# Three quads of eight by seven products in the down projection, with a second set of buffers for the sums of weights

## The chip, the cores and the metric

One core of a Trainium2 chip runs the whole layer in one launch. The metric is the device time in microseconds (us): the median of three runs before the change is 1021.38 us (1021.27 to 1021.45). Engines are named as the profile names them: PE multiplies matrices (PEld is its weight load), DVE is the vector engine, ACT the scalar engine, POOL is GpSimd, SP issues most DMAs. Each engine works through its own instructions in order and waits at semaphores for the others.

## The reference, cut to what matters

A decoder layer in float32 for 256 tokens and a model width of 2048: attention heads and a pooling mixer behind one norm, then a gated MLP with 5632 hidden features. The change concerns the last product of the MLP:

```python
def conv_ffn(h, w_up, conv_w, conv_b, w_down):
    u = h @ w_up
    ...
    gate, val = jnp.split(y, 2, axis=-1)
    return (jax.nn.silu(gate) * val) @ w_down
```

Here `w_down` is 5632 x 2048, and the product is the "down projection"; `h @ w_up` is the "up projection".

## The kernel before, in words

**Three passes per product.** A float32 weight is cut into a high and a low part, both of a type that PE multiplies in one pass. ACT copies the high part (`wh`, L124), DVE subtracts it from the raw weight and keeps the rest (`wl`, L129). Each product is then three matmuls: high by high, high by low, low by high. Every weight of the layer passes through these two copies, so ACT and DVE work all the time for PE.

**Steps.** The work is a list of steps, and each step uses up one half chunk of weights, 128 x 1024. A chunk of 1 MB holds two steps; SP loads it into one of four `raw` buffers, and the next load starts when a buffer is released (`release`, L160). The order of all instructions is written out by the loop at the end of `layer`: at step u it emits the high split of step u + 6 and the low split of step u + 5, and then the matmuls of step u and the actions hooked to it. For a step that belongs to a quad by sums (below) the matmuls come first and the splits after. So on DVE's queue the low split of a step stands five steps ahead of its matmuls, and everything that is emitted between them stands in line with it.

**MLP in thirds.** The hidden features are worked in three thirds of 8, 8 and 6 groups of 256. Of each third first the up projection: per group a gate block and a value block of four steps each, and after the last step of a block DVE and ACT evacuate it (`conv`, L657: `fs`, `u`, `y`), the value block also multiplies by the gate and cuts the result into `hid` (`value`, L679). Then the down projection of that third: two pairs (`down_pair`, L708), each for 1024 of the 2048 output columns.

**Quads.** In a pair, two steps h = 0 and h = 1 form a quad j: two row blocks of 128 hidden features by two column blocks of 512, for two halves of 128 tokens. By the plain way (`quad`, L744) that is eight products, 24 matmuls of 128x512 in two steps of 12. Quads named in `MIXED` go by seven products of sums (`quad_sums`, L727): 12 matmuls in the first step, 9 in the second. These need sums of the tokens' side (`token_sums`, L690: four additions on POOL, a copy on ACT, a subtraction on DVE, into `sx`), formed with the value block of that group, and sums of the weights:

- `seven_sums` (L139), emitted behind the low split of the quad's first step: ACT copies the first 512 columns into `s512h`, DVE makes `s512l` (L150) and then three differences in the raw chunk (L143, L144, L145), the later ones from the earlier.
- One step later `seven_high` has ACT copy the last sum into `s1024h`, and two steps later `seven_low` (L155) has DVE make `s1024l` (L157) and release the chunk.

The high and low parts of these sums are the tiles `s1` (512 wide) and `s4` (1024 wide), one of each before the change. PE reads `s1024l` with the sixth matmul of the quad, and for the last time with the last matmul of its second step.

**PSUM.** The pair's plain sums lie in two `acc` tiles (`box["tok"]`), the seven products in one `aux` tile (two banks, only one buffer exists) and two `small` tiles p5 and p7 (two buffers exist). Behind the last quad by sums, `add_part` 0 to 4 (L778) combine them into `x2`: 0 and 2 copy with ACT (L783) and add in PSUM (L784), 1 and 3 (L786, L789) read `aux`, 4 (L792) reads p5. Behind the last step `close` (L795, L797) adds both `acc` tiles into `x2`. The next pair starts in the same buffers: its first matmul writes `aux`, its fourth group of three writes the `small` buffer that `add_part` 4 has read, and its second step writes the first `acc` tile, which the first copy of `close` has read.

In the third of 8 before the change, quads 0 and 4 go by sums, in the third of 6 quad 0.

Of the kernel before, what the change touches and what calls it, by code (L numbers as in the profile page):

```python
# [25 lines left out]
F32 = mybir.dt.float32  # L26
F32R = mybir.dt.float32r
# [4 lines left out]
P = 128  # L32
# [22 lines left out]
OK = (0, 2, 4, 6, 12, 14, 8, 10)  # L55
V_TILES = [((k, 0), (k, 1)) for k in range(KT - 2)] + [((KT - 2, b), (KT - 1, b)) for b in range(2)]
THIRDS = ((0, 8), (8, 16), (16, 22))
MIXED = {8: (0, 4), 6: (0,)}


def bucket(n):
# [9 lines left out]
def layer(ctx: ExitStack, tc: tile.TileContext, xT, xtok, wts, par, rel_d, ident_d, icnt_d, out):  # L71
    nc = tc.nc
# [20 lines left out]
    def col(c):  # L93
        return pv[:, c:c + 1]


    raws, wparts, shift, late = {}, {}, {}, {}
    seven = set()

    def load(c, pieces=1, j=0):  # L100

# [8 lines left out]
    def raw(u):  # L110
        return raws[u // 2][:, (u % 2) * HALF:(u % 2 + 1) * HALF]
# [27 lines left out]
    def seven_sums(u):  # L139

        w = raws[u // 2]
        both(late["s1"], w[:, :512])
        nc.vector.tensor_tensor(w[:, :1024], w[:, 512:1536], w[:, :1024], op=OP.subtract)  # L143
        nc.vector.tensor_tensor(w[:, 1024:1536], w[:, 1024:1536], w[:, :512], op=OP.subtract)  # L144
        nc.vector.tensor_tensor(w[:, 1536:], w[:, 1536:], w[:, 1024:1536], op=OP.subtract)  # L145

    def both(parts, w, low=True):
        nc.scalar.activation(parts[0], w, AF.Copy)
        if low:
            nc.vector.tensor_tensor(parts[1], w, parts[0].bitcast(F32), op=OP.subtract)  # L150

    def seven_high(u):
        both(late["s4"], raw(u + 1), low=False)

    def seven_low(u):  # L155
        h, l = late["s4"]
        nc.vector.tensor_tensor(l, raw(u + 1), h.bitcast(F32), op=OP.subtract)  # L157
        release(u // 2)

    def release(c):  # L160

        raws.pop(c)
        if c + RAWS < wts.shape[0]:
            load(c + RAWS)
# [334 lines left out]
    steps, hooks = [], []  # L499
# [29 lines left out]
    def feat_block(act, post, alloc=acc):  # L529
        box, runs = {}, []  # L530
        for i, k0 in enumerate(XK):
            def run(u, i=i, k0=k0):
                if i == 0:
                    box["ps"] = alloc("ps_feat")
                feat_half(u, act(), k0, box["ps"], i == 0, i == 3)
                if i == 3:
                    post(box["ps"])
            run.shift = SHIFT
            runs.append([run])
        return runs  # L540

    def after(u, f):

        hooks.append((u, f))
# [22 lines left out]
    for b in range(2):  # L567
# [4 lines left out]
        for j in range(4):  # L572
            h, u = 4 * b + j, at + 2 * j
# [5 lines left out]
            after(at + 7, lambda: st.__setitem__(("T", 1), bias_tile(4)))  # L579


    def open_late():
        ectx.close()
        pool = ctx.enter_context(tc.tile_pool(name="late", bufs=1))
        late["pool"] = pool
        late["x2"] = pool.tile([P, NT, D], F32, name="x2")
        nc.sync.dma_start(late["x2"], xtok)
        late["sx"] = pool.tile([P, 2, 4, 2, P], F32R, name="sx")
        late["s1"], late["s4"] = ([pool.tile([P, n], F32R, name=f"s{n}{p}") for p in "hl"] for n in (512, 1024))
        late["ss"] = pool.tile([P, NT, D // 512], F32, name="ss")  # L590
        late["u"] = [pool.tile([P, 2, 2 + S], F32, name=f"u{i}") for i in range(2)]
        for u in late["u"]:
            nc.gpsimd.memset(u[:, :, :2], 0.0)
# [6 lines left out]
    def residual(ps, b):  # L600
        for t in range(NT):
            x2 = add_to_x2(ps, b, t)
            sq = late["pool"].tile([P, 512], F32, name="xs", tag="y0", bufs=2)
            nc.scalar.activation(sq, x2, AF.Square, accum_out=late["ss"][:, t, b:b + 1])

    def x2_T(b):
# [49 lines left out]

    def conv(ps, f0_, which):  # L657

        pool, u = late["pool"], late["u"][which]
        s = pool.tile([P, 2, S], F32, name="fs", tag="fs", bufs=2)  # L660
        add_halves(s, ps)
        nc.vector.tensor_tensor(u[:, :, 2:], s, late["rrow"][:, None, :].to_broadcast([P, 2, S]), op=OP.mult)  # L662
        y = pool.tile([P, 2, S], F32, name="y", tag=f"y{which}", bufs=2)
        for m in range(2):
            f = f0_ + m
            cw = [col(C_CW + i * 2 * NF + f) for i in range(3)]
            nc.scalar.activation(y[:, m, :], u[:, m, 2:], AF.Identity, scale=cw[2], bias=col(C_CB + f))  # L667
            nc.vector.scalar_tensor_tensor(y[:, m, :], u[:, m, 1:1 + S], cw[1], y[:, m, :],  # L668
                                           op0=OP.mult, op1=OP.add)
            nc.vector.scalar_tensor_tensor(y[:, m, :], u[:, m, :S], cw[0], y[:, m, :],  # L670
                                           op0=OP.mult, op1=OP.add)
        return y
# [6 lines left out]
    def value(ps, g, j):  # L679
        if j == 0:  # L680
            late["hid"] = keep.tile([P, KT, 2, S], F32R, name="hid", tag="c")
        y = conv(ps, NF + 2 * g, 1)
        hid, ks = late["hid"], slice(2 * j, 2 * j + 2)
        nc.vector.tensor_tensor(y, y, late["gate"], op=OP.mult)  # L684
        nc.scalar.activation(hid[:, ks, 0, :], y, AF.Copy)  # L685
        nc.vector.tensor_tensor(hid[:, ks, 1, :], y, hid[:, ks, 0, :].bitcast(F32), op=OP.subtract)
        if j in late["mixed"]:
            token_sums(y, late["mixed"].index(j))
# [14 lines left out]
    def triple(ps, act, w, first, last, skip=False):  # L703

        for n, (a, i) in enumerate(((0, 0), (1, 0), (0, 1))):
            nc.tensor.matmul(ps, act[a], w[i], start=(first and n == 0), stop=(last and n == 2), skip_group_check=skip)  # L706

    def down_pair(bp, nq, final):  # L708


        box, runs, mixed = {}, [], MIXED[nq]
        s_end = 2 * mixed[-1] + 1
        rest = 2 * nq - 1 - s_end

        def hid(k, t):
            return [late["hid"][:, k, a, t * P:(t + 1) * P] for a in range(2)]
# [10 lines left out]
        def quad_sums(u, j, h):  # L727
            if j == 0 and h == 0:
                box["aux"], box["p5"], box["p7"] = aux("ps_p"), small("ps_p5"), small("ps_p7")
                box["tok"] = [acc("ps_down") for t in range(NT)]  # L730
            first, last, i = j == 0, j == mixed[-1], mixed.index(j)
            if h == 0:
                s4, t13 = late["s4"], wparts.pop(u + 1)
                triple(box["aux"][:, 0, :], hid(2 * j, 0), late["s1"], first, last)
                triple(box["aux"][:, 1, :], sums(i, 1), part(s4, 0), first, last)
                triple(box["p5"], sums(i, 0), part(t13, 0), first, last)
                triple(box["p7"], sums(i, 2), part(t13, 1), first, last)
            else:
                b2, s4 = wparts.pop(u - 1), late["s4"]
                triple(bank(0, 1), sums(i, 3), part(b2, 0), first, False, end)  # L740
                triple(bank(0, 0), hid(2 * j + 1, 0), part(b2, 1), first, False, end)
                triple(bank(1, 0), hid(2 * j + 1, 1), part(s4, 1), first, False, end)
# [60 lines left out]
        for j in range(nq):  # L803
            for h in range(2):
                at = 2 * j + h

                def run(u, j=j, h=h, at=at):
                    if j in mixed:
                        quad_sums(u, j, h)
                    elif end and j == nq - 1:  # L810
                        if h == 1:
                            last_quad((u - 1, u), j)
                    else:
                        quad(u, j, h)
                run.seven = j in mixed and h == 0
                acts = [run]
                for n in range(5):
                    if at == s_end + 1 + n * (rest - 1) // 5:
                        acts.append(lambda n=n: add_part(n))
                if at == 2 * nq - 1 and not end:  # L820
                    acts.append(lambda: close(0))
                runs.append(acts)
        return runs

    for n, (g0, g1) in enumerate(THIRDS):
        after(len(steps), lambda nq=g1 - g0: late.__setitem__("mixed", MIXED[nq]))
        for g in range(g0, g1):
            steps += feat_block(lambda: late["h"], lambda ps, g=g: gate(ps, g), aux if n and g == g0 else acc)
            steps += feat_block(lambda: late["h"], lambda ps, g=g, j=g - g0: value(ps, g, j))
        for bp in range(2):  # L830
            steps += down_pair(bp, g1 - g0, n == len(THIRDS) - 1)

    for u, f in hooks:
        steps[u].append(f)
    n = len(steps)
    assert n == 2 * wts.shape[0], (n, wts.shape)
    shift.update((u, getattr(steps[u][0], "shift", 0)) for u in range(n))
    seven.update(u for u in range(n) if getattr(steps[u][0], "seven", False))
    for u in range(n):
        ahead = u + AHEAD + 1  # L840
        pair = (ahead, ahead + 1) if ahead in PAIRS else ()
# [88 lines left out]
```

## Time and profile before

| what | value |
|---|---|
| median of 3 runs | 1021.38 us |
| the profiled execution's own time | 1021.83 us |
| its span, first to last instruction | 1020.0 us |
| busy: PE, DVE, ACT, POOL | 1015.4, 762.5, 542.9, 61.4 us |
| first matmul of the down projection of third 1, 2, 3 | 472.87, 734.76, 952.26 us |

The profile is of one execution. A row of the timeline gives the start in us from the span's start, the duration, the engine, the line, what is written and read, and how many equal instructions follow each other; in brackets stands how long the engine was idle before, and what ended that. Matmuls overlap each other by their fill: a matmul shows 0.39 us and the next one starts 0.23 us later, so PE's work is read from starts, not from durations. The same holds to a smaller degree on DVE. The chain of work gives pieces by their ends, so a start there can lie 0.16 us behind the one in the timeline.

### The profile page before, as it was taken

How to read it: one execution, taken by the hardware profiler on the slowest of the kernel's cores; microseconds unless marked ns; L12 is line 12 of the kernel's file. 1: busy time of each engine (PE TensorE's matmuls, PEld its weight loads, DVE VectorE, ACT ScalarE, POOL GpSimd, SP SyncE). 2: the span in 40 equal slices, each digit the busy share in tenths (PEclk: the TensorE clock that was granted, in tenths of full speed). 3: DMA queues.
4: the chain of work that ended last, by engine and by line, in shares of the span. 5: the costliest groups of instructions: out<-in, count | busy, mean ns of one | idle time of the engine just before them, and what ended most of it. 6: DMA issues, size and time to landing. Idle time of an engine off the chain costs nothing.

```text
span 1020.0 us, 13506 instructions
## 1 busy us (share of the span) xinstructions
PE 1015.4 (100%) x5286; PEld 872.0 (85%) x5286; DVE 762.5 (75%) x958; ACT 542.9 (53%) x729; POOL 61.4 (6%) x74
## 2 busy tenths in 40 slices
PE   9999999999999999999999999999999999999998
PEld 8888888888888888888888888888888888888887
DVE  6956667875567877878987687777889667777893
ACT  6744455554545565555544465555554445564740
POOL 0420004600000000000000000000000000000000
PEclk9999999999999999999999999999999999999999
DMA  9784454475453555444655445546365555445451
GB/s 340 271 281 167 167 182 165 166 289 200 172 181 137 219 196 213 170 166 169 244 212 201 165 177 218 184 169 238 126 249 209 206 178 188 171 173 218 177 216 41
DMA packets 30607, 199.18 MB, mean 195 GB/s; under 512 B 3576, under 2 KB 4472, under 8 KB 7760
## 3 DMA queue, kind: packets, MB, share of 16 engines
q1 hardware_dynamic: 29968, 196.89, 52.7%
q0 software_dynamic: 576, 1.44, 0.7%
q8 instruction: 41, 0.67, 0.3%
q14 instruction: 22, 0.18, 0.0%
HBM read 195.83 MB, written 2.49 MB: 194 GB/s over the span
## 4 chain that ended last, share of the span: by engine, by line
PE 100%; DVE 0%; issue 0%
PE ps_feat L185 35%; PE ps_feat L187 18%; PE ps_down L750 18%; PE ps_tok L172 17%; PE ps_v L179 4%; PE ps_p L706 3%; PE ps_down L706 2%; PE ps_pool L194 1%; PE ps_s L400 1%; PE ps_start L247 0%; PE ps_down L771 0%; PE ps_T L387 0%; PE ps_x2T L615 0%; PE ps_av L433 0%; PE ps_eT L422 0%; PE ps_av L434 0%
## 5 line engine op out<-in xcount | busy, mean ns | idle before, releaser
L129 DVE TENSOR_TENSOR wl<-raw,wh 128x1024 fp32r<-128x1024 f32 x358 | 436.0, 1253 | 80.0 <-PE ps_tok L172 27.7
L185 PE MATMUL ps_feat<-x2h,wh 128*128 128x512 f32 x1408 | 488.6, 392 | 0.0
L124 ACT ACTIVATE wh<-raw 128x1024 fp32r<-128x1024 f32 x358 | 362.1, 1051 | 159.1 <-DVE raw L143 44.2
L187 PE MATMUL ps_feat<-x2h,wl 128*128 128x256 f32 x1408 | 393.6, 280 | 0.0
L185 PEld LDWEIGHTS ps_feat<-x2h,wh 128*128 128x128 f32 x1408 | 264.3, 188 | 58.3
L187 PEld LDWEIGHTS ps_feat<-x2h,wl 128*128 128x128 f32 x1408 | 264.3, 188 | 0.1
L750 PE MATMUL ps_down<-wh,hid 128*128 128x512 f32 x528 | 130.4, 389 | 0.0
L750 PEld LDWEIGHTS ps_down<-wh,hid 128*128 128x128 f32 x528 | 99.1, 188 | 20.6
L667 ACT ACTIVATE y<-u,pv 128x256 f32<-128x256 f32 x88 | 48.2, 595 | 70.6 <-DVE u L662 70.6
L750 PE MATMUL ps_down<-wl,hid 128*128 128x512 f32 x264 | 70.6, 389 | 0.0
L172 PE MATMUL ps_tok<-wh,xh 128*128 128x512 f32 x256 | 70.1, 396 | 0.0
L172 PE MATMUL ps_tok<-wh,cat 128*128 128x512 f32 x256 | 68.8, 390 | 0.0
L668 DVE SCALAR_TENSOR_TENSOR y<-u,pv,y 128x256 f32<-128x256 f32 x88 | 42.4, 482 | 29.6 <-ACT y L667 29.6
L450 DVE TENSOR_TENSOR fs<-ps_feat,fs 128x512 f32<-128x512 f32 x44 | 30.4, 691 | 38.1 <-ACT fs L449 38.1
L750 PEld LDWEIGHTS ps_down<-wl,hid 128*128 128x128 f32 x264 | 49.6, 188 | 10.3
L172 PEld LDWEIGHTS ps_tok<-wh,cat 128*128 128x128 f32 x256 | 47.6, 188 | 9.6
L172 PEld LDWEIGHTS ps_tok<-wh,xh 128*128 128x128 f32 x256 | 47.5, 188 | 9.4
L449 ACT ACTIVATE fs<-ps_feat 128x512 f32<-128x512 f32 x44 | 26.2, 595 | 44.6 <-PE ps_feat L187 44.4
L185 PE MATMUL ps_feat<-xh,wh 128*128 128x512 f32 x128 | 46.2, 402 | 0.0
L670 DVE SCALAR_TENSOR_TENSOR y<-u,pv,y 128x256 f32<-128x256 f32 x88 | 42.7, 485 | 3.1
L699 POOL TENSOR_TENSOR s<-y 128x128 f32<-128x128 f32 x10 | 6.0, 597 | 629.8 <-DVE y L684 629.8
L685 ACT ACTIVATE hid<-y 128x512 fp32r<-128x512 f32 x22 | 14.0, 634 | 49.0 <-DVE y L684 49.0
(173 smaller groups left out, 904.4 us busy)
## 6 DMA issues: line engine op xcount, KB each, us to landing
raw<-in_wts SPq DMA_DIRECT2D x177, 1024.0 KB, 4.9
raw<-in_wts SPq DMA_DIRECT2D x4, 512.0 KB, 7.9
x<-in_xtok SPq DMA_DIRECT2D x1, 2048.0 KB, 9.6
raw<-in_wts SPq DMA_DIRECT2D x7, 256.0 KB, 5.5
xboth<-in_xT SPq DMA_DIRECT2D x4, 256.0 KB, 6.9
T<-band POOLq DMA_DIRECT2D x8, 128.0 KB, 7.8
out<-x SPq DMA_DIRECT2D x2, 512.0 KB, 6.4
out<-x SPq DMA_DIRECT2D x3, 256.0 KB, 2.2
```

The lines of the kernel that those rows point to most:

```text
L124: nc.scalar.activation(wparts[u][0], raw(u - 1 if u - 1 in seven else u + 1 if u in seven else u), AF.Copy)
L129: nc.vector.tensor_tensor(wl, raw(u - 1 if u - 1 in seven else u + 1 if u in seven else u), wh.bitcast(F32), op=OP.subtract)
L172: nc.tensor.matmul(ps[:, t, :], act[:, k0 + k, a, t * P:(t + 1) * P], w[:, k * 512:(k + 1) * 512], start=(first and k == 0 and n == 0), st ...
L179: nc.tensor.matmul(ps[:, t, :], act[:, k, a, t * P:(t + 1) * P], w[i], start=(first and n == 0), stop=(last and n == 2))
L185: nc.tensor.matmul(ps, wh[:, ws], act[:, k, :, :], start=(first and n == 0), stop=False, skip_group_check=True)
L187: nc.tensor.matmul(ps[:, S:], wl[:, ws], act[:, k, 0, :], start=False, stop=(last and n == len(ks) - 1), skip_group_check=True)
L450: nc.vector.tensor_tensor(dst, ps[:, :, :S], dst, op=OP.add)
L667: nc.scalar.activation(y[:, m, :], u[:, m, 2:], AF.Identity, scale=cw[2], bias=col(C_CB + f))
L668: nc.vector.scalar_tensor_tensor(y[:, m, :], u[:, m, 1:1 + S], cw[1], y[:, m, :], op0=OP.mult, op1=OP.add)
L670: nc.vector.scalar_tensor_tensor(y[:, m, :], u[:, m, :S], cw[0], y[:, m, :], op0=OP.mult, op1=OP.add)
L706: nc.tensor.matmul(ps, act[a], w[i], start=(first and n == 0), stop=(last and n == 2), skip_group_check=skip)
L750: nc.tensor.matmul(bank(t, b), hid(2 * j + h, t)[a], part(w, b if h == 0 else 1 - b)[i], start=(t == b == 1 and j == 1 and h == 0 and n == ...
```

## The change

In thirds of 8 the quads 0, 3 and 5 now go by seven products (before 0 and 4), in the third of 6 quads 0 and 3 (before 0). There are now two sets of `s1` and `s4`, used in turn. The second set has its place in a pool "temps" which during the up projection holds the temporaries `fs`, `y` and `xs`, and which is closed and opened anew at each passage from up to down projection and back. `sx` holds three quads' token sums in place of two. The scratch area for POOL's DMAs is half as large. The five `add_part` calls stand between the last quad by sums and the last step: before in steps 10 to 14 of 16 (third of 6: steps 2 to 10 of 12), now in steps 12, 12, 13, 13, 14 (third of 6: steps 8, 8, 9, 9, 10).

```diff
-MIXED = {8: (0, 4), 6: (0,)}
+MIXED = {8: (0, 3, 5), 6: (0, 3)}
...
     def seven_sums(u):
 
         w = raws[u // 2]
-        both(late["s1"], w[:, :512])
+        both(late["s"][seven[u]][0], w[:, :512])
...
     def seven_high(u):
-        both(late["s4"], raw(u + 1), low=False)
+        both(late["s"][seven[u]][1], raw(u + 1), low=False)
...
+    def seven_tiles(pool, i):
+        return [[pool.tile([P, n], F32R, name=f"s{n}{p}{i}") for p in "hl"] for n in (512, 1024)]
+
+    def open_temps(down):
+
+        if "ctx" in late:
+            late["ctx"].close()
+        late["ctx"] = ExitStack()
+        late["temps"] = late["ctx"].enter_context(tc.tile_pool(name="temps", bufs=1))
+        if down:
+            late["temps"].tile([P, 72], F32, name="row")
+            late["s"][1] = seven_tiles(late["temps"], 1)
...
-        late["sx"] = pool.tile([P, 2, 4, 2, P], F32R, name="sx")
-        late["s1"], late["s4"] = ([pool.tile([P, n], F32R, name=f"s{n}{p}") for p in "hl"] for n in (512, 1024))
+        late["sx"] = pool.tile([P, 3, 4, 2, P], F32R, name="sx")
+        late["s"] = [seven_tiles(pool, 0), None]
+        open_temps(False)
...
-                run.seven = j in mixed and h == 0
+                run.seven = (len(mixed) * bp + mixed.index(j)) % 2 if j in mixed and h == 0 else None
...
+        after(len(steps) - 1, lambda: open_temps(True))
         for bp in range(2):
             steps += down_pair(bp, g1 - g0, n == len(THIRDS) - 1)
+        after(len(steps) - 1, lambda n=n: open_temps(False) if n < len(THIRDS) - 1 else late["ctx"].close())
...
-    nc = bacc.Bacc("TRN2", target_bir_lowering=False, num_devices=1, dynamic_dma_scratch_size=8192)
+    nc = bacc.Bacc("TRN2", target_bir_lowering=False, num_devices=1, dynamic_dma_scratch_size=4096)
```

By the built programs, PE has 18 matmuls fewer (5243 to 5225), DVE 33 additions and subtractions more, ACT 15 copies more and POOL 12 additions more.

On DVE, third 1, first pair, directly behind the evacuation of the last value block (`hid`): the low splits of steps 5 and following, and the sums of the second quad by sums. Before:

```order
L686 TENSOR_TENSOR hid<-y,hid 128x2x256
L129 TENSOR_TENSOR wl<-raw,wh 128x1024 x4
L150 TENSOR_TENSOR s512l<-raw,s512h 128x512
L143 TENSOR_TENSOR raw<-raw 128x1024
L144 TENSOR_TENSOR raw<-raw 128x512
L145 TENSOR_TENSOR raw<-raw 128x512
L129 TENSOR_TENSOR wl<-raw,wh 128x1024 x2
L157 TENSOR_TENSOR s1024l<-raw,s1024h 128x1024
L129 TENSOR_TENSOR wl<-raw,wh 128x1024 x5
```

The same place now, on to the sums of the third quad by sums (`s512l_4133` and `s1024l_4135` are the second set, `s512l_1872` and `s1024l_1874` the first):

```order
L700 TENSOR_TENSOR hid<-y,hid 128x2x256
L129 TENSOR_TENSOR wl<-raw,wh 128x1024 x2
L150 TENSOR_TENSOR s512l_4133<-raw,s512h_4132 128x512
L143 TENSOR_TENSOR raw<-raw 128x1024
L144 TENSOR_TENSOR raw<-raw 128x512
L145 TENSOR_TENSOR raw<-raw 128x512
L129 TENSOR_TENSOR wl<-raw,wh 128x1024 x2
L157 TENSOR_TENSOR s1024l_4135<-raw,s1024h_4134 128x1024
L129 TENSOR_TENSOR wl<-raw,wh 128x1024 x2
L150 TENSOR_TENSOR s512l_1872<-raw,s512h_1871 128x512
```

The sums for the second quad stand two low splits earlier than before, and one more set of sums follows.

On DVE, the end of the same pair: from the sums for the next pair's first quad to `close`. Before:

```order
L150 TENSOR_TENSOR s512l<-raw,s512h 128x512
L143 TENSOR_TENSOR raw<-raw 128x1024
L144 TENSOR_TENSOR raw<-raw 128x512
L145 TENSOR_TENSOR raw<-raw 128x512
L786 TENSOR_TENSOR x_1868<-ps_p,x_1868 128x1024
L129 TENSOR_TENSOR wl<-raw,wh 128x1024
L784 TENSOR_TENSOR ps_p<-ps_p,s 128x512
L129 TENSOR_TENSOR wl<-raw,wh 128x1024
L157 TENSOR_TENSOR s1024l<-raw,s1024h 128x1024
L789 TENSOR_TENSOR x_1868<-ps_p,x_1868 128x1024
L129 TENSOR_TENSOR wl<-raw,wh 128x1024
L792 TENSOR_TENSOR x_1868<-ps_p_4118,x_1868 128x2x512
```

And now, from the low split behind those sums:

```order
L129 TENSOR_TENSOR wl<-raw,wh 128x1024
L798 TENSOR_TENSOR ps_p<-ps_p,s 128x512
L800 TENSOR_TENSOR x_1868<-ps_p,x_1868 128x1024
L129 TENSOR_TENSOR wl<-raw,wh 128x1024
L157 TENSOR_TENSOR s1024l_4135<-raw,s1024h_4134 128x1024
L798 TENSOR_TENSOR ps_p<-ps_p,s 128x512
L803 TENSOR_TENSOR x_1868<-ps_p,x_1868 128x1024
L129 TENSOR_TENSOR wl<-raw,wh 128x1024
L806 TENSOR_TENSOR x_1868<-ps_p_4137,x_1868 128x2x512
L129 TENSOR_TENSOR wl<-raw,wh 128x1024
L811 TENSOR_TENSOR x_1868<-ps_down,x_1868 128x1024 x2
```

Before, `add_part` 0 (L784) stood ahead of the next pair's sums; now all five parts (L798 to L806) stand behind them, and `close` (L811) behind those.

More of the change, by code (lines that the diff above doesn't have):

```diff
@@ L97, in layer @@
     raws, wparts, shift, late = {}, {}, {}, {}
-    seven = set()
+    seven = {}
     def load(c, pieces=1, j=0):
@@ L152, in seven_high @@
     def seven_high(u):
-        both(late["s4"], raw(u + 1), low=False)
+        both(late["s"][seven[u]][1], raw(u + 1), low=False)
     def seven_low(u):
-        h, l = late["s4"]
+        h, l = late["s"][seven[u]][1]
         nc.vector.tensor_tensor(l, raw(u + 1), h.bitcast(F32), op=OP.subtract)
@@ L602, in residual @@
             x2 = add_to_x2(ps, b, t)
-            sq = late["pool"].tile([P, 512], F32, name="xs", tag="y0", bufs=2)
+            sq = late["temps"].tile([P, 512], F32, name="xs", tag="y0", bufs=2)
             nc.scalar.activation(sq, x2, AF.Square, accum_out=late["ss"][:, t, b:b + 1])
@@ L657, in conv @@
     def conv(ps, f0_, which):
-        pool, u = late["pool"], late["u"][which]
+        pool, u = late["temps"], late["u"][which]
         s = pool.tile([P, 2, S], F32, name="fs", tag="fs", bufs=2)
@@ L732, in quad_sums @@
             if h == 0:
-                s4, t13 = late["s4"], wparts.pop(u + 1)
-                triple(box["aux"][:, 0, :], hid(2 * j, 0), late["s1"], first, last)
+                (s1, s4), t13 = late["s"][seven[u]], wparts.pop(u + 1)
+                triple(box["aux"][:, 0, :], hid(2 * j, 0), s1, first, last)
                 triple(box["aux"][:, 1, :], sums(i, 1), part(s4, 0), first, last)
@@ L738, in quad_sums @@
             else:
-                b2, s4 = wparts.pop(u - 1), late["s4"]
+                b2, s4 = wparts.pop(u - 1), late["s"][seven[u - 1]][1]
                 triple(bank(0, 1), sums(i, 3), part(b2, 0), first, False, end)
@@ L837, in layer @@
     shift.update((u, getattr(steps[u][0], "shift", 0)) for u in range(n))
-    seven.update(u for u in range(n) if getattr(steps[u][0], "seven", False))
+    seven.update((u, i) for u, i in ((u, getattr(steps[u][0], "seven", None)) for u in range(n)) if i is not None)
     for u in range(n):
```

## The prediction

> **What bounds the kernel now.** I read the page first, then the chain of work that ended last, then busy time by stage, then the timelines of PE and DVE around one pair. On the page, busy time by engine and the chain's shares:
>
> ```profile
> PE 1015.4 (100%) x5286; PEld 872.0 (85%) x5286; DVE 762.5 (75%) x958; ACT 542.9 (53%) x729; POOL 61.4 (6%) x74
> PE 100%; DVE 0%; issue 0%
> ```
>
> PE bounds the kernel: it waits for nobody, and a matmul less is time saved, unless another engine is then late. The windows are third 1's up projection, its first pair and its second (length; busy us of PE, PEld, DVE, ACT, POOL, with instructions):
>
> ```profile
> 302.00:473.00 171.00, 171.00 (x988) 150.56 (x987) 133.25 (x173) 95.09 (x124) 4.43 (x8) 1.00 0.50 182
> 473.00:515.00 42.00, 42.00 (x187) 34.73 (x186) 38.47 (x42) 24.61 (x30) 0.00 (x0) 1.00 0.59 221
> 515.00:557.50 42.50, 42.50 (x190) 35.18 (x189) 31.88 (x30) 19.54 (x21) 0.00 (x0) 1.00 0.62 227
> ```
>
> DVE's 75% is an average over stages. In the first pair it is busy 38.47 of 42.00 us, since the last value block's evacuation falls into it. That is the stage to cost. Its timeline of PE (start, duration):
>
> ```profile
> 472.87 0.63 PE L706 MATMUL ps_p<-s512h,hid 128*128 128x512 f32 x2
> 474.03 0.39 PE L706 MATMUL ps_p<-s1024l,sx 128*128 128x512 f32 x1
> 477.70 1.98 PE L750 MATMUL ps_down<-wh,hid 128*128 128x512 f32 x8
> 480.42 1.98 PE L750 MATMUL ps_down<-wh,hid 128*128 128x512 f32 x8
> 494.02 0.62 PE L706 MATMUL ps_p<-s512h,hid 128*128 128x512 f32 x2
> 495.15 0.39 PE L706 MATMUL ps_p<-s1024l,sx 128*128 128x512 f32 x1
> 498.78 1.98 PE L750 MATMUL ps_down<-wh,hid 128*128 128x512 f32 x8
> 515.10 0.62 PE L706 MATMUL ps_p<-s512h,hid 128*128 128x512 f32 x2
> 517.82 0.62 PE L706 MATMUL ps_down<-wh,sx 128*128 128x512 f32 x2
> ```
>
> and of DVE, with a row of ACT:
>
> ```profile
> 472.55 1.22 DVE L157 TENSOR_TENSOR s1024l<-raw,s1024h 128x1024 fp32r<-128x1024 f32 x1
> 481.99 4.62 DVE L129 TENSOR_TENSOR wl<-raw,wh 128x1024 fp32r<-128x1024 f32 x4
> 486.53 0.69 DVE L150 TENSOR_TENSOR s512l<-raw,s512h 128x512 fp32r<-128x512 f32 x1
> 487.25 1.22 DVE L143 TENSOR_TENSOR raw<-raw 128x1024 f32<-128x1024 f32 x1
> 489.84 2.35 DVE L129 TENSOR_TENSOR wl<-raw,wh 128x1024 fp32r<-128x1024 f32 x2
> 492.12 1.22 DVE L157 TENSOR_TENSOR s1024l<-raw,s1024h 128x1024 fp32r<-128x1024 f32 x1
> 493.25 3.49 DVE L129 TENSOR_TENSOR wl<-raw,wh 128x1024 fp32r<-128x1024 f32 x3
> 503.56 1.22 DVE L143 TENSOR_TENSOR raw<-raw 128x1024 f32<-128x1024 f32 x1
> 507.76 0.58 ACT L783 ACTIVATE s<-ps_p 128x512 f32<-128x512 f32 x1
> 515.83 2.35 DVE L797 TENSOR_TENSOR x<-ps_down,x 128x1024 f32<-128x1024 f32 x2
> ```
>
> PE's margin over DVE is small: `s1024l` of the first quad ends at 472.55 + 1.22 = 473.77 and is read at 474.03, 0.26 us later; for the second quad 493.34 against 495.15, 1.81 us. At the pair's end the first `close` copy ends about 517.05 (515.83 + 1.22, as of other whole copies), and its bank is written at 517.82.
>
> **The matmuls removed.** A step of 12 matmuls takes 480.42 - 477.70 = 2.72 us, 0.227 us each; a quad by sums 498.78 - 494.02 = 4.76 us for 21, a plain one 5.44. One more quad by sums in each of six pairs removes 18 matmuls: 0.68 us a pair, 1.36 a third, 4.08 in all. The Trainium skill, "TensorE: Matmul & The Clock Gate", section Back-to-back issue gap, states a warm gap of N / 2.4 + 2.5 ns, 216 ns for 512 columns; by it the saving were 3.88 us and the forecast 0.2 us higher. The row decides.
>
> **What DVE has to do more.** From those rows, start to start: a low split (4.62 - 1.22) / 3 = 1.14 us; the four sums 489.84 - 486.53 = 3.31; `s1024l` 493.25 - 492.12 = 1.13. An extra quad by sums adds 4.44 us of DVE to a pair. The first pair's 38.47 becomes 42.9 of 41.3 us: DVE is then the slower one there. So I follow DVE's queue in its new order from 481.99, where it has just left the evacuation:
>
> - Second quad (now 3): two low splits to 484.27, sums to 487.58, two low splits to 489.86, `s1024l` ends 491.08. PE reaches that quad after one product quad (4.83, 477.70 - 472.87) and two plain ones, 488.58, and reads `s1024l` 1.13 later, at 489.71. With 0.03 us from end to start (L150's end 487.22 to L143's 487.25), **PE waits 1.40 us.**
> - Third quad (5): DVE goes on at 490.99, two splits, sums, two splits, `s1024l` ends 500.08. PE, moved by the wait, reads it at 488.58 + 1.40 + 4.76 + 5.44 + 1.13 = 501.31. No wait.
> - Behind it DVE has four low splits to 504.55, the next pair's sums to 507.86 and a split to 509.00. Then `add_part` 0 needs ACT's copy, which stands behind ACT's splits, and these wait for L143. In the rows the copy ended 507.76 + 0.58 - (503.56 + 1.22) = 3.56 us after L143; now L143 ends 504.55 + 1.94 (488.47 - 486.53) = 506.49, so the addition starts at 510.08, 1.08 us idle.
> - From there, at 0.72 for a half addition that the next waits for and 1.13 for a whole one (prices of L150 to L143, and of L157): add 0, add 1, split, `s1024l`, add 2, add 3 ends 516.14; split, add 4 ends 518.41; split, first `close` copy ends 520.68.
> - PE begins pair 2 at 515.10 - 0.68 + 1.40 = 515.82. Its first matmul writes `aux`: until 516.17, **0.35**. Nine matmuls later (2.04) the fourth group needs p5's buffer: from 518.21 to 518.44, **0.23**. Its second step needs the first `acc` tile: from 519.12 to 520.71, **1.59**.
>
> Together 3.57 us of waits against 1.36 saved: **+2.21 us** a third. Check: PE's second step of pair 2 moves from 517.82 to 520.71, +2.89, and pair 2 saves 0.68 later. From there PE gains: pair 2 carries no evacuation, and its 31.88 plus 4.44 fit its 41.8 us.
>
> Third 3, the same places:
>
> ```profile
> 952.26 0.63 PE L706 MATMUL ps_p<-s512h,hid 128*128 128x512 f32 x2
> 961.39 3.49 DVE L129 TENSOR_TENSOR wl<-raw,wh 128x1024 fp32r<-128x1024 f32 x3
> 986.98 0.62 PE L706 MATMUL ps_down<-wh,sx 128*128 128x512 f32 x2
> ```
>
> There are two quads by sums in the pair, and the five additions follow two steps behind the second. DVE from 961.39: two splits, sums, two splits, `s1024l` ends 970.48 (wait 1.41 as above); four splits, the next sums and a split to 979.40; ACT's copy 980.45; additions, splits and `s1024l` as above, the first `close` copy ends 991.08. PE's second step of pair 2 starts 991.11 in place of 986.98: +4.13, less 0.68, **+3.45 us**. In this third the additions stood spread over the pair before; now they stand in DVE's late stretch.
>
> **Sum:** 2 x 2.21 + 3.45 = +7.87 us (waits 11.95, saved 4.08) on the profiled execution's 1021.83: 1029.7. The median lies 0.45 lower: **1029.2 us.**
>
> **What I cost at nothing.** Token sums: one more per third, and the last one group later. Rows of them and of DVE's idle time behind group 5's place:
>
> ```profile
> L701 DVE TENSOR_TENSOR sx<-s,sx 128x512 fp32r<-128x512 f32 x5 | 3.5, 692 | 8.0 <-ACT sx L700 8.0
> 440.42 0.69 DVE L450 TENSOR_TENSOR fs<-ps_feat,fs 128x512 f32<-128x512 f32 x1 [0.42 <-ACT fs L449]
> 451.51 0.69 DVE L450 TENSOR_TENSOR fs<-ps_feat,fs 128x512 f32<-128x512 f32 x1 [1.94 <-ACT fs L449]
> ```
>
> One costs DVE 0.69 and a wait of 8.0 / 5 = 1.60; 0.42 + 1.94 = 2.36 us of idle time hide 2.29, so the start at 481.99 stands, with no margin. POOL's 12 additions lie where POOL is busy 4.43 of 171 us. The second set's first writer waits for readers of `y` that DVE has passed by then. The halved scratch could delay POOL's DMAs:
>
> ```profile
> 65.46 2.19 POOL L308 DMA_DIRECT2D T<-band x4 [10.15 <-DMA band<-rsb]
> L405 DVE CUSTOM_DVE_ANT_0 e<-ps_s,T x16: 276/353/424, 107.1 to 181.8; 128x128 f32<-128x128 f32 x8, 128x256 f32<-128x256 f32 x8
> ```
>
> 41 us lie between issue and first use. All tiles move by 4 KB or so; no row shows an address effect, so I leave it at nothing, either way.
>
> **Rivals.** *The products alone:* PE is the bound and its buffers of five steps hold, 4.08 saved, 1017.3 us. For it speaks 100% against 75%. The Trainium skill, "Perfetto Trace Analysis", section Identifying the Most-Contended Engine, has one optimize first the engine with the highest occupancy, for PE by weight-load time; the 85% of PEld name PE here too, and by that rule the change gains. Against it: DVE must be 1.40 us earlier at quad 3 and 1.6 at the pair's end, where it is busy 38.47 of 42.00 us already. *Only quad 3 waits:* DVE catches up by the pair's end because ACT's copy isn't waited for and the splits run closer: 3 x 1.40 - 4.08 = +0.1, 1021.5 us; decided by whether add 3 and `close` end before PE comes, 1.6 us earlier than I find. *A late start:* the token sums' 2.29 us stay in DVE's queue up to 481.99. Then every wait above grows by it, and already the first quad with its 0.26 us waits: 3 x 2.29 = 6.9 more, 1036 us; decided by the idle rows at 440 and 451.
>
> **How the numbers follow.** 85% for the forecast's case, 5% each for the rivals. A measurement here tells some 0.2%, 2 us, from no change. The forecast's own bounds: ACT's copy may come early (1.08 x 3 lower, 1026.0), or a part of the token sums stays (0.9 each, 1032). The range is 1026.0 to 1032.0; about 3% of the 85 lie outside it. Faster 5%, same 5%, slower 90%.
>
> **What would show it.** After: PE waits for DVE in the list of waits, some 12 us in all: `s1024l` in the second quad of each first pair (1.4 us each), and `aux` and the first `acc` tile at the start of each second pair (0.4 and 1.6; in third 3 1.6 and 1.6). DVE without idle time in the first pairs, matmuls that start 0.227 us apart as before. Wrong would be no PE wait at quad 3, or waits at the first quad of a third.

## The result, and the profile after

The changed kernel takes 1029.79 us (median of 4 runs, 1029.67 to 1029.9) against 1021.36 us before: ratio 1.0083, 95% interval 1.0065 to 1.0100. It is 8.43 us slower; the forecast was 1029.2 us, 7.87 us slower. The profiled execution has a span of 1028.0 us, 8.0 more than before. Busy time by engine and the chain's shares:

```profile
PE 1014.7 (99%) x5268; PEld 867.2 (84%) x5268; DVE 790.3 (77%) x991; ACT 551.4 (54%) x744; POOL 67.9 (7%) x86
PE 89%; DVE 7%; issue 2%; ACT 1%; DVEq 0%; ACTq 0%
```

The 18 matmuls are gone (5286 to 5268 in the trace). By starts they are 4.08 us, yet PE is only 0.7 us less busy by this sum: a matmul that stands ahead of a wait counts with its whole duration, and those beside a wait start further apart (rows below). What says more is the second line: 7% of the path that sets the end now runs through DVE, where before all of it was PE. Whom PE waited for (us in total, times, longest):

```profile
PE ps_down L720 <- DVE x L811: 3.7, 3, 1.2
PE ps_p L720 <- DVE s1024l L157: 3.2, 3, 1.1
PE ps_p L720 <- DVE x L803: 1.5, 2, 1.4
PE ps_start L247 <- DVE ones L244: 1.1, 1, 1.1
```

Each third has one wait for `s1024l` and one for `close` (L811), and two of three show one for `add_part` 3 (L803); the wait at the start was there before. The list counts from the modelled end of a matmul, which lies 0.16 us or more behind the point at which the next could start, so the waits are larger by starts. PE in third 1, the rows that answer to those of before:

```profile
472.46 0.63 PE L720 MATMUL ps_p<-s512h,hid 128*128 128x512 f32 x2
473.63 0.39 PE L720 MATMUL ps_p<-s1024l,sx 128*128 128x512 f32 x1
...
488.14 0.62 PE L720 MATMUL ps_p<-s512h,hid 128*128 128x512 f32 x2
488.60 0.39 PE L720 MATMUL ps_p<-s512l,hid 128*128 128x512 f32 x1
488.89 0.73 PE L720 MATMUL ps_p<-s1024h,sx 128*128 128x512 f32 x2
490.69 0.50 PE L720 MATMUL ps_p<-s1024l,sx 128*128 128x512 f32 x1 [1.07 <-DVE s1024l L157]
491.03 0.63 PE L720 MATMUL ps_p<-wh,sx 128*128 128x512 f32 x2
...
515.85 0.70 PE L720 MATMUL ps_p<-s512h,hid 128*128 128x512 f32 x2 [0.15 <-DVE x L803]
...
518.12 0.70 PE L720 MATMUL ps_p<-wh,sx 128*128 128x512 f32 x2
518.66 0.39 PE L720 MATMUL ps_p<-wl,sx 128*128 128x512 f32 x1
520.29 0.73 PE L720 MATMUL ps_down<-wh,sx 128*128 128x512 f32 x2 [1.25 <-DVE x L811]
520.87 0.39 PE L720 MATMUL ps_down<-wl,sx 128*128 128x512 f32 x1
```

and DVE there:

```profile
481.57 2.35 DVE L129 TENSOR_TENSOR wl<-raw,wh 128x1024 fp32r<-128x1024 f32 x2
483.84 0.68 DVE L150 TENSOR_TENSOR s512l<-raw,s512h 128x512 fp32r<-128x512 f32 x1
...
489.43 1.22 DVE L157 TENSOR_TENSOR s1024l<-raw,s1024h 128x1024 fp32r<-128x1024 f32 x1
...
509.62 0.70 DVE L798 TENSOR_TENSOR ps_p<-ps_p,s 128x512 f32<-128x512 f32 x1 [1.00 <-ACT s L797]
...
514.48 1.22 DVE L803 TENSOR_TENSOR x<-ps_p,x 128x1024 f32<-128x1024 f32 x1
...
519.02 2.35 DVE L811 TENSOR_TENSOR x<-ps_down,x 128x1024 f32<-128x1024 f32 x2
```

DVE leaves the evacuation at 481.57 and has one gap, 1.00 us for ACT's copy, up to the end of `close`. PE's starts behind the two long waits follow an end on DVE by 0.05 us or less: 489.43 + 1.22 = 490.65 and 490.69, 519.02 + 1.22 = 520.24 and 520.29. Behind `add_part` 3 it is 0.15 us: 514.48 + 1.22 = 515.70 and 515.85.

From one third's first product to the next's, PE takes 736.68 - 472.46 = 264.22 us (before 734.76 - 472.87 = 261.89), then 956.56 - 736.68 = 219.88 (before 217.50), and from there to the end 71.44 (before 67.74): +2.33, +2.38 and +3.70. The stretch ahead of the first third is 0.41 us shorter in this execution. The rows from which the second and third are read:

```profile
736.68 0.63 PE L720 MATMUL ps_p<-s512h,hid 128*128 128x512 f32 x2
956.56 0.63 PE L720 MATMUL ps_p<-s512h,hid 128*128 128x512 f32 x2
```

### The profile page after: what moved, and what is told of

The parts are those of the page before. It is cut to its first block, busy times and chain, and to the rows that moved or that the text cites. A ratio compares the mean times of both kernels' runs of the same rounds, so it can differ in the third digit from the quotient of the medians.

```text
span 1028.0 us, 13533 instructions
## 1 busy us (share of the span) xinstructions
PE 1014.7 (99%) x5268; PEld 867.2 (84%) x5268; DVE 790.3 (77%) x991; ACT 551.4 (54%) x744; POOL 67.9 (7%) x86
## 4 chain that ended last, share of the span: by engine, by line
PE 89%; DVE 7%; issue 2%; ACT 1%; DVEq 0%; ACTq 0%
PE ps_feat L185 34%; PE ps_feat L187 17%; PE ps_tok L172 17%; PE ps_down L764 8%; PE ps_v L179 4%; PE ps_p L720 3%; DVE wl L129 3%; PE ps_down L720 2%; DVE s1024l L157 1%; DVE raw L143 1%; PE ps_pool L194 1%; PE ps_s L400 1%; ACT wh L124 0%; PE ps_start L247 0%; PE ps_down L785 0%
## 5 line engine op out<-in xcount | busy, mean ns | idle before, releaser
L764 PE MATMUL ps_down<-wh,hid 128*128 128x512 f32 x432 | 106.7, 389 | 0.0
L764 PEld LDWEIGHTS ps_down<-wh,hid 128*128 128x128 f32 x432 | 81.1, 188 | 16.9
L764 PE MATMUL ps_down<-wl,hid 128*128 128x512 f32 x216 | 57.7, 389 | 0.0
L713 POOL TENSOR_TENSOR s<-y 128x128 f32<-128x128 f32 x16 | 10.1, 632 | 694.0 <-DVE y L698 392.0
L764 PEld LDWEIGHTS ps_down<-wl,hid 128*128 128x128 f32 x216 | 40.5, 188 | 8.4
```

Source lines behind the costliest of these rows:

```text
L764: nc.tensor.matmul(bank(t, b), hid(2 * j + h, t)[a], part(w, b if h == 0 else 1 - b)[i], start=(t == b == 1 and j == 1 and h == 0 and n == ...
```

## The experiments

My theory was the forecast's: DVE's queue in the first pairs, with its extra and earlier sums, makes PE wait at quad 3 and at the start of the next pair (for `aux`, for p5's buffer and for the first `acc` tile). The rivals: the new places of the buffers and the pool's passages cost the time; an extra quad by sums costs alike wherever it stands; the waits come from ACT, from transfers or from buffers and not from DVE's work; the order on DVE doesn't matter, only its amount.

**The buffers alone.**

```diff
-MIXED = {8: (0, 3, 5), 6: (0, 3)}
+MIXED = {8: (0, 4), 6: (0,)}
```

> All of the change but the extra quads: two sets of sums' buffers, the pool opened and closed, halved scratch, all tiles moved, and the old places (0, 4) and (0). Theory (DVE's extra work in the first pairs makes PE wait): nothing is lost here, 1021.4 us, no wait of PE beyond the one at its start. Rival (the buffers' new places or the pool's passages cost the time): near 1029.8 us.

Measured 1021.0 us against 1021.33, ratio 0.9998 (0.9989 to 1.0007), and no wait of PE but that at its start. The buffers, the passages of the pool, the halved scratch and the moved tiles cost nothing that can be measured; the whole loss comes with the number and the places of the quads by sums.

**The extra quad in the first pairs alone.** The table names the quads of each pair, and `down_pair` takes those of its own:

```diff
-MIXED = {8: (0, 3, 5), 6: (0, 3)}
+MIXED = {8: ((0, 3, 5), (0, 3)), 6: ((0, 3), (0,))}
...
-        box, runs, mixed = {}, [], MIXED[nq]
+        box, runs, mixed, all_ = {}, [], MIXED[nq][bp], max(MIXED[nq], key=len)
```

> The extra quad by sums only in the first pair of each third; the second pair has as many as before ((0, 3) and (0)). Theory: all waits of the change stay, and only half of the saving: 1029.8 + 3 x 0.68 = 1031.8 us. Rival (each extra quad costs alike, wherever it stands): half of the loss of 8.4, 1025.6 us.

Measured 1032.09 us, ratio 1.0104 (1.0090 to 1.0118). It is slower than the changed kernel although it does half of the extra quads: all waits of the first pairs are there, with nearly the same totals as above (3.7, 3.2 and 1.6 us in the list), and the second pairs' 2.04 us are no longer saved. That the cost is the same for each quad is excluded.

**The extra quad in the second pairs alone,** once with late and once with early token sums. The first:

```diff
+MIXED = {8: ((0, 4), (0, 4, 6)), 6: ((0,), (0, 3))}
...
```

> The extra quad only in the second pairs: first pairs (0, 4) and (0) as before, second pairs (0, 4, 6) and (0, 3). Token sums are now made with group 6 of 8, the last but one. Theory with the token sums in DVE's line: the second pairs have room (saved 2.0), but the 2.29 us of group 6's token sums find only 0.24 us of idle time before the last evacuation ends, so DVE starts about 2.05 late and PE waits 2.05 - 0.26 = 1.8 us at the first quad of the two thirds of 8: 1021.4 - 2.0 + 3.6 = 1022.9 us. If token sums cost nothing: 1019.3. If second pairs have no room either: 1025 or more.

Measured 1025.62 us (four runs, 1024.63 to 1026.22), ratio 1.0044 (1.0028 to 1.0059), 2.7 us more than expected. By the time alone the third case of the expectation, second pairs without room (1025 or more), fits better. The trace excludes it: apart from its start, PE waits at the first quad of the two thirds of 8 and nowhere else, so not in the second pairs. Third 1:

```profile
472.89 0.63 PE L720 MATMUL ps_p<-s512h,hid 128*128 128x512 f32 x2
474.82 0.73 PE L720 MATMUL ps_p<-s1024h,sx 128*128 128x512 f32 x2 [1.07 <-ACT s1024h L148]
476.27 0.50 PE L720 MATMUL ps_p<-s1024l,sx 128*128 128x512 f32 x1 [0.72 <-DVE s1024l L157]
...
496.37 0.62 PE L720 MATMUL ps_p<-s512h,hid 128*128 128x512 f32 x2
```

From the first quad to the second it is 23.48 us, before 494.02 - 472.87 = 21.15: 2.33 us a third in place of the expected 1.8. DVE at group 6's token sums, with a row of ACT:

```profile
456.97 0.99 DVE L700 TENSOR_TENSOR hid<-y,hid 128x512 fp32r<-128x512 f32 x1 [0.70 <-ACT hid L699]
459.41 0.69 DVE L715 TENSOR_TENSOR sx<-s,sx 128x512 fp32r<-128x512 f32 x1 [1.44 <-ACT sx L714]
460.02 4.63 DVE L129 TENSOR_TENSOR wl<-raw,wh 128x1024 fp32r<-128x1024 f32 x4
...
466.62 1.06 ACT L124 ACTIVATE wh<-raw 128x1024 fp32r<-128x1024 f32 x1 [3.88 <-DVE raw L143]
468.20 0.69 DVE L450 TENSOR_TENSOR fs<-ps_feat,fs 128x512 f32<-128x512 f32 x1 [0.24 <-ACT fs L449]
```

From the start of `hid` to the next split it is 3.05 us, without token sums 481.57 - 480.96 = 0.61 (changed kernel): they cost 2.44 us, not 2.29. And the 0.24 us of idle time that I had counted as a reserve is still there at 468.20: it is a wait for ACT's copy, and that copy stands behind a split of ACT (466.62) which itself waits for DVE's L143, so it has moved along. So DVE is 2.44 us late, and PE, with 0.26 us of margin, waits about 2.2. Two thirds of 2.33, less 2.04, make +2.6, and the span is 2.7 longer than before (1022.7 against 1020.0). The median of the four runs is 1 us further up than the profiled execution, 1024.63. Single runs of the kernel before scatter by about that (1020.68 to 1021.94); beside this, the three longer runs have a mean granted clock of PE of 0.998, the profiled one of 1.000. No trace shows where in them the clock was lower.

The second, with quads 0, 3 and 4, so that no token sums are made later than group 4:

```diff
+MIXED = {8: ((0, 4), (0, 3, 4)), 6: ((0,), (0, 3))}
...
```

> As the run before, but second pairs of (0, 3, 4) in the thirds of 8, so that no token sums are made later than group 4; third of 6 (0) and (0, 3). Theory: nine matmuls removed (1.5 quads' worth of the saving: three pairs at 0.68), no wait of PE anywhere, 1021.4 - 2.0 = 1019.3 us, faster than both kernels. Rival (every extra quad makes PE wait): 1021.4 or more.

Measured 1019.29 us (11 runs), ratio 0.9982 (0.9973 to 0.9990): 2.04 us faster than the kernel before, as expected, from nine matmuls at 0.227 us. The list of waits has PE's start alone, and DVE's load fits. Here are the first and the second pair of third 1 (length; busy us of PE, PEld, DVE, ACT, POOL, with instructions; granted clock, DMA share, GB/s):

```profile
473.00:515.00 42.00, 42.00 (x187) 34.82 (x186) 38.52 (x42) 24.66 (x30) 0.00 (x0) 1.00 0.61 230
515.00:557.50 42.50, 42.50 (x192) 35.30 (x191) 36.56 (x36) 20.01 (x22) 0.00 (x0) 1.00 0.60 218
```

The second pair's DVE went from 31.88 to 36.56 us and stays below PE's 42.50. This version beats both kernels.

**More work for DVE, in both kernels.** The last subtraction of the evacuation (`hid` low) of each third's last value block is done three times:

```diff
+        if j == late["nq"] - 1:
+            for _ in range(2):
+                nc.vector.tensor_tensor(hid[:, ks, 1, :], y, hid[:, ks, 0, :].bitcast(F32), op=OP.subtract)
...
```

> The kernel before, with the last subtraction of the last value block's evacuation (hid low) done three times in place of once: about 2 x 0.7 = 1.4 us more DVE work ahead of each first pair, the same output. Theory: the second quad's margin of 1.81 us and the idle time behind it take it up, 1021.4 us (up to 0.3 more). If DVE is as tight before as after: + 3 x 1.4 = 4.2, 1025.6 us.

Measured 1021.22 us, ratio 0.9999 (0.9990 to 1.0009). DVE is late here too, but not too late for PE. The second quad's `s1024l` ends at 493.01 + 1.22 = 494.23, and PE reads it at 494.57:

```profile
493.01 1.22 DVE L157 TENSOR_TENSOR s1024l<-raw,s1024h 128x1024 fp32r<-128x1024 f32 x1
494.57 0.39 PE L709 MATMUL ps_p<-s1024l,sx 128*128 128x512 f32 x1
```

> The changed kernel with the same two extra subtractions per third. Theory: DVE's queue sets the first pairs from quad 3 to the first close copy, so each us more there is a us more in the time: 1029.8 + 3 x 1.4 = 1034.0 us. Rival (PE's waits come from ACT, from transfers or from the buffers, DVE has room): about 1029.8.

Measured 1034.18 us, ratio 1.0134 (1.0118 to 1.0149). In the trace the extra work delays the next split by 482.81 - 481.47 = 1.34 us, and the three stretches from first product to first product (the last to the end) are 1.48, 1.45 and 1.40 us longer than in the changed kernel:

```profile
481.47 1.42 DVE L703 TENSOR_TENSOR hid<-y,hid 128x512 fp32r<-128x512 f32 x2
482.81 2.35 DVE L129 TENSOR_TENSOR wl<-raw,wh 128x1024 fp32r<-128x1024 f32 x2
```

At quad 3 the wait is now in two parts, 4.0 us in all for ACT's `s1024h` and 3.2 for `s1024l`. ACT's copy stands behind splits that wait for DVE's L143 (3.50 us in third 1), so this part too goes back to DVE. The same work at the same place costs nothing before the change, and afterwards its full length and a little more. This is the most direct evidence that DVE's queue sets the first pairs of the changed kernel, and that it didn't before.

**Close first.** Two low splits that stand ahead of `add_part` 4 and `close` are emitted behind them, with no work added or taken:

```diff
+                run.hold = bp == 0 and at >= 2 * nq - 2
+                run.free = bp == 0 and at == 2 * nq - 1
...
+            if getattr(steps[u][0], "hold", False):
+                held.append(ahead - 1)
+            else:
+                split_low(ahead - 1)
...
+        if getattr(steps[u][0], "free", False):
+            while held:
+                split_low(held.pop(0))
```

> The changed kernel with one change of order: in the last two steps of each first pair the two low splits are emitted behind close in place of ahead of it (same work). Theory: add 4 and close come 1.14 and 2.28 us earlier on DVE, the waits of 0.23 and 1.59 us at the fourth group and the second step of pair 2 go, those at quad 3 and at aux stay: 1029.8 - 3 x 1.82 = 1024.3 us. Rival (the time is DVE's total work, whatever its order): 1029.8.

Measured 1024.6 us, ratio 1.0031 (1.0019 to 1.0042), 5.2 us less than the changed kernel; 5.5 were expected. In its list PE waits for `s1024l` as in the changed kernel (3.2 us), once for `add_part` 3 (1.4, in third 3), and no longer for `close`. Two waits of 0.2 us, at the first matmul of pair 2 in thirds 1 and 2, are put down to ACT's `wh`. In third 1 `add_part` 3 ends at 515.27 and PE starts at 515.41, about as far behind it as in the changed kernel, so this is more likely what is left of the wait for `aux`. So PE waits for particular instructions in DVE's line, and where they stand in it matters as well as how much work there is. It does not make the extra quads of the first pairs worth while: the wait at quad 3 alone is more than a pair saves.

**The third of 6 alone.**

```diff
-MIXED = {8: (0, 3, 5), 6: (0, 3)}
+MIXED = {8: (0, 4), 6: (0, 3)}
```

> The changed kernel with the old places (0, 4) in the thirds of 8, and (0, 3) in the third of 6 only. Theory: the terms are per third, here the third's own one of +3.45 by the forecast (3.7 as the changed kernel's trace has it): 1021.4 + 3.5 to 3.7 = 1024.9 to 1025.1 us. Rival (equal loss in each third): 1021.4 + 2.8 = 1024.2.

Measured 1025.18 us against 1021.38, ratio 1.0037 (1.0023 to 1.0051): +3.8. By the trace it is 1023.6 - 952.23 = 71.37 us from the third's first product to the end, 3.63 more than before.

```profile
PE ps_p L720 <- DVE x L803: 1.4, 1, 1.4
PE ps_down L720 <- DVE x L811: 1.2, 1, 1.2
PE ps_p L720 <- DVE s1024l L157: 1.1, 1, 1.1
```

The waits are those of the changed kernel's third 3, one of each kind: this third loses alone what it loses in the changed kernel (3.70).

## Why the prediction was right, step by step

**The saving** was sized rightly: matmuls start 0.227 us apart as before, and nine of them removed without a wait gave 2.04 us in the run with quads (0, 3, 4).

**The wait at quad 3.** Forecast 1.40 us a third; by starts it is 490.69 - (488.14 + 1.13) = 1.42. In the thirds of 8 it comes from the place of the second quad and not from the third one, since no work was added on DVE between the evacuation and that quad's `s1024l`. Moved from quad 4 to quad 3, the tile is read two steps earlier (5.44 us) and stands only two low splits earlier on DVE (2.27 us): of the margin of 1.81 us before, 1.81 - (5.44 - 2.27) = -1.36 is left. No run has (0, 3) or (0, 4, 6) in a first pair, so what a third quad alone would cost there is not shown.

**`aux` and p5's buffer.** Forecast 0.35 and 0.23 in third 1; measured about 0.3 (515.85, where PE would have started near 515.54) and 0.1 (518.12 against 518.01). Two things differ from the forecast. PE came 0.13 us later. And its starts lie 0.14 to 0.15 us behind DVE's ends at both places, where the forecast had 0.03: at p5's buffer DVE is done at 517.98, before PE could have started, and PE starts at 518.12. Why this distance is larger than at `s1024l` and `close` (0.05) is not shown.

**The first `close` copy.** Forecast to end at 520.68, and with the stretch ahead 0.41 us shorter at 520.27; it ended at 520.24. The queue, worked out item by item over 39 us, was 0.03 us off. (Its low splits were taken at 1.14 us, where the quotient given for them is 1.133; two of them took 2.27.) The wait behind it was 1.40 in place of 1.59, again because PE came later.

**ACT's copy** kept DVE idle for 1.00 us (forecast 1.08).

**What was left out.** Behind each wait PE loses about 0.1 us more: 491.03 - 490.69 is 0.34 in place of 0.23, 520.87 - 520.29 is 0.58 for two matmuls in place of 0.45. As long as DVE is the later one that is swallowed by the next wait, but not behind the last: this 0.13 explains the difference of third 1 (+2.33 against +2.21) and most of third 2's. Of third 3's (+3.70 against +3.45) about 0.1 us stays without a place. These are the 0.5 us by which the sum fell short.

**The list of waits** was forecast at some 12 us and shows 8.4 without the start. This is in part an error in how I read that view, which counts from the modelled ends. By starts the waits are 3.24, 3.26 and 4.44 us, 10.9 in all. The other 1.6 of the 12.5 us that PE loses (8.41 + 4.08) are the slower starts beside the waits, which the forecast had at nothing.

**The token sums.** I let them hide, with no margin. By the run with quad 6 they cost 2.44 us, not 2.29: the subtraction of `hid` is itself slower beside POOL's additions, 1.00 us in place of 0.69. That is more than the 2.36 us of idle time counted on, and that they hid all the same is in part luck. In the changed kernel DVE starts the evacuation behind them late and the one after that on time, with no idle time ahead of either:

```profile
434.35 1.00 DVE L700 TENSOR_TENSOR hid<-y,hid 128x512 fp32r<-128x512 f32 x1 [0.70 <-ACT hid L699]
436.79 0.69 DVE L715 TENSOR_TENSOR sx<-s,sx 128x512 fp32r<-128x512 f32 x1 [1.44 <-ACT sx L714]
437.40 4.62 DVE L129 TENSOR_TENSOR wl<-raw,wh 128x1024 fp32r<-128x1024 f32 x4
441.94 0.68 DVE L450 TENSOR_TENSOR fs<-ps_feat,fs 128x512 f32<-128x512 f32 x1
...
451.10 0.69 DVE L450 TENSOR_TENSOR fs<-ps_feat,fs 128x512 f32<-128x512 f32 x1
```

Here 451.10 is the 451.51 of before, less 0.41. Without idle time ahead of it, a piece of DVE's work starts 0.08 us before the one ahead has ended (437.40 + 4.62 = 442.02, and 441.94), and at two places this made up for the 0.08 us that were missing. The rival of a late start was therefore near, and the run with quad 6 shows what it looks like.

**The rivals.** The products alone (1017.3 us) fell with the waits, and so did quad 3 as the only wait, since `aux` and the first `acc` tile were waited for too. The rule that the engine with the highest occupancy should be relieved first, from the Trainium skill's "Perfetto Trace Analysis", section Identifying the Most-Contended Engine, would have pointed to a gain. The Trainium skill's "Perfetto Trace Analysis", section Optimization Strategy, says that the most contended engine can change over time, and that is what this trace has: over the whole span PE leads by 100% to 75%, and in the first pair of each third margins of 0.26 us (first quad), 1.81 us (second quad) and 0.77 us (the first `close` copy) decide.

## What to carry to other kernels

When an engine is relieved at the cost of another, cost it in the stage where that other one is busiest, and follow its queue in order from the last point at which it is known to be on time: the margin of each reader (0.26, 1.81 and 0.77 us here before the change), not the share of busy time, tells what fits. Work that is only moved can use up a margin too: at quad 3 an earlier place was enough, by the count above. The same extra work can be free in one stage and cost its full length in the next, so move it there: the extra quads in the second pairs alone gave 2.04 us when their token sums were made early, and those in the first pairs lost over 10. Idle time behind a wait for a third engine is not a reserve if that engine waits for the first one.

## What the runs showed of the hardware that I had not expected

**A clock that falls without a long pause.** In the changed kernel with more work for DVE, in third 3, PE waited twice within 4 us, and the matmuls behind that are slow for a while:

```profile
975.40 0.39 PE L723 MATMUL ps_p<-s512l,hid 128*128 128x512 f32 x1
977.14 0.73 PE L723 MATMUL ps_p<-s1024h,sx 128*128 128x512 f32 x2 [1.35 <-ACT s1024h L148]
978.96 0.80 PE L723 MATMUL ps_p<-s1024l,sx 128*128 128x512 f32 x1 [1.08 <-DVE s1024l L157]
979.55 1.05 PE L723 MATMUL ps_p<-wh,sx 128*128 128x512 f32 x2
```

Windows of 2 us (length; busy PE; granted clock, DMA share, GB/s):

```profile
975.00:977.00 2.00, 0.79 (x4) 1.00 0.15 61
977.00:979.00 2.00, 0.77 (x3) 0.85 0.00 0
979.00:981.00 2.00, 2.00 (x5) 0.50 0.47 115
981.00:983.00 2.00, 2.00 (x9) 0.80 0.93 381
983.00:985.00 2.00, 2.00 (x11) 1.00 0.85 303
```

The granted clock goes to 0.50 and back within 6 us. The Trainium skill, "TensorE: Matmul & The Clock Gate", section Part 1, has the clock halved after an idle window of about 3.4 us; here no pause in the rows was longer than 1.35 us, and PE was busy for 1.56 of 4 us. In thirds 1 and 2 of the same execution the same waits, with PE busy for 1.59 of 4 us, left the clock at 1.00; what makes the difference is not shown. It cost no time in this execution, whose third 3 grew by 1.40 us and the others by 1.48 and 1.45, since DVE's `close` came later still. One run of that kernel, at a mean clock of 0.994, took 1037.18 us where the others took 1033.88 to 1034.36; of that run there is no trace.

**DVE beside POOL.** The subtraction that gives `hid` (two inputs of 128x512) takes 0.69 us. Where it starts while one of POOL's additions for the token sums runs, it takes 0.93 to 1.00 us, as at group 0 of third 1 and, in third 1 of all kernels here, at every later group with token sums. Where it starts first, by 0.01 us, it keeps its 0.69 us and POOL's addition takes 1.01 us in place of 0.46, here at group 0 of third 2 before the change:

```profile
585.72 0.69 DVE L686 TENSOR_TENSOR hid<-y,hid 128x512 fp32r<-128x512 f32 x1 [0.70 <-ACT hid L685]
585.73 1.01 POOL L699 TENSOR_TENSOR s<-s,y 128x128 f32<-128x128 f32 x1
```

So the two hold each other up, and the later one pays. The Trainium skill, "GPSIMD Engine Reference", section Specifications, names the interface that both share when DVE reads two SBUF inputs; the trace agrees.
